# Order of the three matmuls of a split product: per tile, or per piece of weights (one hybrid attention and HGRN2 layer, one Trainium2 core)

## Chip, cores and metric

One core of a Trainium2 chip runs the whole program. The metric is device time in microseconds (us) for one launch, the median of several runs. A difference of 0.2% is about 5.9 us here.

## What is computed

One layer of a bidirectional encoder, 1024 tokens of width 2048, all in float32:

```
u = rmsnorm(h, g_pre)
z = u @ w_in
aq, ak, av, ag, hq, hf_f, hf_b, hv, hg = jnp.split(z, SPLIT_IDX, axis=-1)
...
y = jnp.concatenate([y_att, y_hg], axis=-1).astype(h.dtype) @ w_out
h = h + rmsnorm(y, g_post)
gate = jax.nn.sigmoid((h @ w_pg).astype(f32))
e = (p_l @ w_pp).astype(f32)
h = h + rmsnorm((gate * e).astype(h.dtype), g_ple)
```

Here w_in is 2048 x 9216, w_out and w_pg are 2048 x 2048, w_pp is 256 x 2048. Between the first two products stand a dilated banded attention of 16 heads and a two-directional HGRN2 scan of 8 heads.

## The kernel before

**The split product.** Every large product is made of three matmuls. An activation tile is kept as hi (fp32r) and lo (bf16, the remainder), a weight piece as wh (fp32r), wl (fp32r, the remainder) and wb (bf16). The product is hi·wh + hi·wl + lo·wb, added up in one PSUM bank. Such three matmuls, each of 512 columns, are called a triple below, the two fp32r ones H, the bf16 one B. There are 3392 triples. An H carries its weight load inside its own instruction; a B has an instruction LDWEIGHTS of its own ahead of it.

**The pieces.** `piece` (L74 to L85) loads 128 rows x 512 columns of weights (or 4 x 128 x 128) into raw, and ScalarE makes wh (L82), GpSimd wl (L83, in some pieces VectorE), VectorE wb (L84). raw, wh, wl and wb have three buffers each, so the parts of later pieces are made while TensorE works on earlier ones.

**Who uses pieces.** In `group_parts` (L92 to L106) the weights are the stationary operand: one group makes 128 columns of z for both halves of the tokens, in 4 pieces, and each piece serves 2 halves x 4 k-tiles = 8 triples. It is a generator: it yields after each half, so that attention can put other work between. There are 56 groups, so 224 pieces. In `v_group` (L728 to L741) the tokens' tiles are the stationary operand: 16 pieces per call, with one triple per token tile, 2, 2 and 4 tiles in the first three calls and 8 in the last three. In `gemm` (L798 to L823), which makes w_out, w_pg and w_pp products for half of the tokens, a piece serves 4 token tiles; its last `tail` pieces (1, and 8 in the very last call) are kept back, and then run tile by tile, each tile's bank being read out as soon as it is complete.

**Stages.** First the prenorm, the transposes and the v groups (to about 395 us); then 8 HGRN heads (to about 1270 us), each of 4 groups and a chain of small matmuls that takes turns with VectorE (`hgrn`, L272, L278, L297, L304, L349, L363); then 8 pairs of attention heads (to about 2085 us), each with a k, a q and a gate group and 16 units of scores (L631, L636), softmax (L642 to L650), transposes (L655) and products with v (L539, L553); then w_out, and at last w_pg with w_pp, the second rmsnorm and the output.

**Order.** TensorE runs its instructions in the order of its queue. That order is made when the kernel is built: a scheduler works through the program in the order of its lines with priorities (pieces come early), and puts small matmuls of the chains between the triples of a group where it expects their inputs.

Of the kernel before, what the change touches and what calls it, by code (L numbers as in the profile page):

```python
# [24 lines left out]
KT = 16  # L25
# [19 lines left out]
class Kern:  # L45
# [17 lines left out]

    # ---- weights: a piece [128 (k), 512] in three parts
    def gb(self):
# [20 lines left out]

    # ---- z^T for 128 columns of w_in
    def group(self, *a):
# [3 lines left out]
    def group_parts(self, w_in, c0, sink, halves=(0, 1)):  # L92
        nc = self.nc
        pb = {hf: self.gb() for hf in halves}
        for p in range(4):
            src = w_in[512 * p:512 * p + 512, c0:c0 + 128].rearrange("(k p) c -> p k c", p=128)
            wh, wl, wb = self.piece(src, [4, 128])
            for hf in halves:
                for k in range(4):
                    kt = 4 * p + k  # L100
                    nc.tensor.matmul(pb[hf], wh[:, k], self.uh[hf][:, kt], start=(kt == 0), stop=False)  # L101
                    nc.tensor.matmul(pb[hf], wl[:, k], self.uh[hf][:, kt], start=False, stop=False)  # L102
                    mm = nc.tensor.matmul(pb[hf], wb[:, k], self.ul[hf][:, kt], start=False, stop=(kt == KT - 1))  # L103
                yield mm
        for hf in halves:
            sink(hf, pb[hf])  # L106
# [36 lines left out]

    # ---- split of x^T-like data held in PSUM into hi and lo
    def split_evac(self, hi, lo, p):
# [4 lines left out]

    # ---- phase 0
    def prenorm(self, x, g_pre, pool, tiles):
# [19 lines left out]

    # ---- HGRN2
    def hg_consts(self, lbs, g_hg):
# [50 lines left out]
    def hgrn(self, w_in, h, vsrc, yout):  # L225
# [21 lines left out]

        # ---- intra-chunk scores
        X = big.tile([128, S], F32, name="X", tag="X", bufs=2)
# [13 lines left out]
        n = S  # L263
# [144 lines left out]

    # ---- attention
    def att_consts(self, positions):  # L410
# [292 lines left out]
def tile_hybrid(ctx, tc, x, p, positions, w_in, w_out, g_pre, g_post, g_hg, lb_fwd, lb_bwd, w_pg, w_pp, g_ple, out):  # L703
# [22 lines left out]
    def v_group(cg, toks, pool):  # L726
        c0 = (2048, 2560, 7168, 7680)[cg]
        pb = {t: (K.gb() if t < NGB else K.wk("vb")) for t in toks}  # L728
        for k in range(KT):
            wh, wl, wb = K.piece(w_in[128 * k:128 * k + 128, c0:c0 + 512], [512], prio=False,  # L730
                                 sub=V if len(toks) == 2 and k % 2 else None)
            for t in toks:
                ts = slice(128 * (t % 4), 128 * (t % 4) + 128)
                hi, lo = K.uh[t // 4], K.ul[t // 4]
                nc.tensor.matmul(pb[t], hi[:, k, ts], wh, start=(k == 0), stop=False)  # L735
                nc.tensor.matmul(pb[t], hi[:, k, ts], wl, start=False, stop=False)
                nc.tensor.matmul(pb[t], lo[:, k, ts], wb, start=False, stop=(k == KT - 1))  # L737
        for t in toks:
# [58 lines left out]
    def gemm(w, act, order, c0, sink, tail, bank, pre=None, get=None):  # L797
# [5 lines left out]

        def mm(t, k, pc, first, last):
            ts = slice(128 * t, 128 * t + 128)
            wh, wl, wb = pc
            nc.tensor.matmul(pb[t], hi[:, k, ts], wh, start=first, stop=False)  # L807
            nc.tensor.matmul(pb[t], hi[:, k, ts], wl, start=False, stop=False)  # L808
            nc.tensor.matmul(pb[t], lo[:, k, ts], wb, start=False, stop=last)  # L809

        for j, k in enumerate(order):
            if pre:
                pre(j, k)
            pc = K.piece(w[128 * k:128 * k + 128, c0:c0 + 512], [512], get(j) if get else None)
            if j < n - tail:
                for t in toks:
                    mm(t, k, pc, j == 0, False)
            else:
                pcs.append((k, pc))
        for t in toks:  # L820
            for i, (k, pc) in enumerate(pcs):
                mm(t, k, pc, n == tail and i == 0, i == len(pcs) - 1)
            sink(t, pb[t])  # L823
# [195 lines left out]
```

## Time and profile before

| | |
|---|---|
| runs | 2932.80, 2936.83, 2938.66 us; median 2936.83 |
| profiled execution | its span is 2936.8 us; the profile gives no other time of it |
| TensorE (PE) busy | 2842.3 us, 97% of the span |
| weight loads (PEld) busy | 1684.8 us, 57% |
| VectorE (DVE) busy | 1433.9 us, 49% |
| GpSimd (POOL) busy | 1046.8 us, 36% |
| ScalarE (ACT) busy | 930.2 us, 32% |

A row of the view of groups gives a line of the kernel, the engine, the operation, output<-inputs by the program's names, the shape, how often it occurs, then the busy time, the mean of one in ns, and the idle time of the engine just before them with what ended it. A row of the timeline gives start and duration in us, engine, line and operation; instructions of one line in a row are merged, with their count behind x. Matmuls overlap in these rows, since each row includes the way through the array: what a matmul costs the engine is the distance between the ends (or starts) of two neighbours, not its duration.

### The profile page before, as it was taken

The numbers are of one execution on the slowest core, as the hardware profiler recorded it, in microseconds if no ns is written. First come the engines' busy times: TensorE is split into PE (matmuls) and PEld (weight loads), VectorE is DVE, ScalarE is ACT, GpSimd is POOL, SyncE is SP. The second block draws the span as 40 slices with busy tenths as digits, with TensorE's granted clock in tenths as the row PEclk, the third lists the DMA queues.
The fourth block names the chain that finished last, engine by engine and source line by source line (L and its number), as shares of the span: only waits on it lengthen the run. The fifth ranks groups of instructions, "written<-read, shape, count | busy, mean of one in ns | idle before, by whom it ended". The sixth has DMA issues, their size and how long they took to land. (4 is left out here: it accounts for less than half of the span.)

```text
span 2936.8 us, 46862 instructions
## 1 busy us (share of the span) xinstructions
PE 2842.3 (97%) x18384; PEld 1684.8 (57%) x18384; DVE 1433.9 (49%) x2833; ACT 930.2 (32%) x1676; POOL 1046.8 (36%) x769
## 2 busy tenths in 40 slices
PE   6999999999999999999999999999999999999997
PEld 4555556566566566565555555555555555555554
DVE  8501116756255355356656556565632633543435
ACT  5311112222122122124434434443533223333323
POOL 2422224324314313322222222222244554666555
PEclk9999999999999999999999999999999999999999
DMA  6412221211211111122221222222344543443443
GB/s 229 121 49 76 76 86 37 65 52 37 59 50 40 59 48 41 58 58 62 74 70 43 77 72 56 59 74 70 103 125 127 161 146 94 124 121 108 143 153 113
DMA packets 251613, 250.54 MB, mean 85 GB/s; under 512 B 21632, under 2 KB 175232, under 8 KB 250240
## 3 DMA queue, kind: packets, MB, share of 16 engines
q1 hardware_dynamic: 242224, 238.62, 27.5%
q10 hardware_dynamic: 9168, 8.93, 0.9%
q8 instruction: 144, 2.36, 0.3%
q14 instruction: 77, 0.63, 0.1%
HBM read 205.54 MB, written 29.36 MB: 80 GB/s over the span
## 5 line engine op out<-in xcount | busy, mean ns | idle before, releaser
L83 POOL TENSOR_TENSOR wl<-raw,wh 128x512 fp32r<-128x512 f32 x568 | 786.5, 1389 | 1590.5 <-ACT wh L82 1496.4
L101 PE MATMUL gb<-uh,wh 128*128 128x512 f32 x1792 | 1027.9, 574 | 0.0
L84 DVE CAST wb<-raw 128x512 bf16<-128x512 f32 x584 | 346.8, 598 | 955.7 <-PE gb L103 377.4
L82 ACT CAST wh<-raw 128x512 fp32r<-128x512 f32 x584 | 358.5, 618 | 1190.8 <-PE gb L101 343.9
L102 PE MATMUL gb<-uh,wl 128*128 128x512 f32 x1792 | 711.1, 397 | 1.0 <-POOL wl L83 1.0
L103 PE MATMUL gb<-ul,wb 128*128 128x512 bf16 x1792 | 698.8, 390 | 0.0
L103 PEld LDWEIGHTS <-wb 128*128 128x128 bf16 x1792 | 172.1, 96 | 467.9 <-issue 460.5
L102 PEld LDWEIGHTS gb<-uh,wl 128*128 128x128 f32 x1792 | 340.6, 190 | 44.1 <-POOL wl L83 1.4
L101 PEld LDWEIGHTS gb<-uh,wh 128*128 128x128 f32 x1792 | 358.6, 200 | 3.5 <-issue 1.5
L807 PE MATMUL gb<-wh,yh 128*128 128x512 f32 x512 | 296.1, 578 | 2.9 <-DVE Y L833 2.0
L807 PE MATMUL gb<-wh,th 128*128 128x512 f32 x480 | 277.3, 578 | 0.0
L808 PE MATMUL gb<-wl,yh 128*128 128x512 f32 x512 | 203.5, 398 | 3.2 <-POOL wl L83 3.2
L809 PE MATMUL gb<-wb,yl 128*128 128x512 bf16 x512 | 201.0, 393 | 0.0
L808 PE MATMUL gb<-wl,th 128*128 128x512 f32 x480 | 190.9, 398 | 5.9 <-POOL wl L83 5.7
L809 PE MATMUL gb<-wb,tl 128*128 128x512 bf16 x480 | 187.3, 392 | 0.0
L735 PE MATMUL gb<-wh,uh 128*128 128x512 f32 x256 | 146.6, 579 | 2.1 <-ACT wh L82 2.1
L735 PE MATMUL vb<-wh,uh 128*128 128x512 f32 x256 | 148.4, 580 | 0.0
L647 ACT ACTIVATE asm<-asm,anm 128x512 f32<-128x512 f32 x128 | 92.5, 723 | 147.8 <-DVE anm L645 147.0
L809 PEld LDWEIGHTS <-yl 128*128 128x128 bf16 x512 | 49.3, 96 | 138.0 <-issue 137.7
L737 PEld LDWEIGHTS <-ul 128*128 128x128 bf16 x512 | 49.2, 96 | 137.8 <-issue 137.0
L809 PEld LDWEIGHTS <-tl 128*128 128x128 bf16 x512 | 49.0, 96 | 136.7 <-issue 136.3
L642 DVE CUSTOM_DVE_ANT_1 asm<-asc,amask 128x512 f32<-128x512 f32 x128 | 87.8, 686 | 76.0 <-PE asc L636 75.9
(274 smaller groups left out, 3958.4 us busy)
## 6 DMA issues: line engine op xcount, KB each, us to landing
raw<-in_w_in_dram SPq DMA_DIRECT2D x320, 256.0 KB
raw<-in_w_out_dram SPq DMA_DIRECT2D x128, 256.0 KB
raw<-in_w_pg_dram SPq DMA_DIRECT2D x128, 256.0 KB
xt<-in_x_dram SPq DMA_DIRECT2D x8, 1024.0 KB
vD<-vo SPq DMA_DIRECT2D x32, 256.0 KB
raw<-yD SPq DMA_DIRECT2D x32, 256.0 KB
xr<-in_x_dram SPq DMA_DIRECT2D x32, 256.0 KB
ak<-ak SPq DMA_DIRECT2D x96, 64.0 KB
```

Source lines behind the costliest of these rows:

```text
L82: nc.scalar.copy(wh, raw)
L83: (sub or nc.gpsimd).tensor_tensor(wl, raw, f32(wh), op=ALU.subtract)
L84: nc.vector.tensor_copy(wb, raw)
L101: nc.tensor.matmul(pb[hf], wh[:, k], self.uh[hf][:, kt], start=(kt == 0), stop=False)
L102: nc.tensor.matmul(pb[hf], wl[:, k], self.uh[hf][:, kt], start=False, stop=False)
L103: mm = nc.tensor.matmul(pb[hf], wb[:, k], self.ul[hf][:, kt], start=False, stop=(kt == KT - 1))
L642: V.tensor_tensor_reduce(out=smh.rearrange("p (a b) -> p a b", a=2), in0=sc.rearrange("p (a b) -> p a b", a=2), in1=mk, scale=1.0, scalar= ...
L647: nc.scalar.activation(smh, smh, AF.Exp, bias=nm, accum_out=den)
L735: nc.tensor.matmul(pb[t], hi[:, k, ts], wh, start=(k == 0), stop=False)
L807: nc.tensor.matmul(pb[t], hi[:, k, ts], wh, start=first, stop=False)
L808: nc.tensor.matmul(pb[t], hi[:, k, ts], wl, start=False, stop=False)
L809: nc.tensor.matmul(pb[t], lo[:, k, ts], wb, start=False, stop=last)
```

## The change

In each piece the H of all tiles are issued first, and the B of all tiles behind them. In `group_parts` that makes 16 H and then 8 B; the generator's first yield comes behind 16 H and 4 B, its second behind 4 more B. In `v_group` it makes 2 H per token tile and then one B per tile. In `gemm` it makes 8 H and then 4 B; in the kept-back part each tile runs the H of all kept pieces, and then their B. No instruction is added or taken away, and no operand changes.

```diff
@@ group_parts
             for hf in halves:
                 for k in range(4):
                     kt = 4 * p + k
                     nc.tensor.matmul(pb[hf], wh[:, k], self.uh[hf][:, kt], start=(kt == 0), stop=False)
                     nc.tensor.matmul(pb[hf], wl[:, k], self.uh[hf][:, kt], start=False, stop=False)
+            for hf in halves:
+                for k in range(4):
+                    kt = 4 * p + k
                     mm = nc.tensor.matmul(pb[hf], wb[:, k], self.ul[hf][:, kt], start=False, stop=(kt == KT - 1))
                 yield mm
@@ v_group
             for t in toks:
-                ts = slice(128 * (t % 4), 128 * (t % 4) + 128)
-                hi, lo = K.uh[t // 4], K.ul[t // 4]
-                nc.tensor.matmul(pb[t], hi[:, k, ts], wh, start=(k == 0), stop=False)
-                nc.tensor.matmul(pb[t], hi[:, k, ts], wl, start=False, stop=False)
-                nc.tensor.matmul(pb[t], lo[:, k, ts], wb, start=False, stop=(k == KT - 1))
+                hi = K.uh[t // 4][:, k, 128 * (t % 4):128 * (t % 4) + 128]
+                nc.tensor.matmul(pb[t], hi, wh, start=(k == 0), stop=False)
+                nc.tensor.matmul(pb[t], hi, wl, start=False, stop=False)
+            for t in toks:
+                lo = K.ul[t // 4][:, k, 128 * (t % 4):128 * (t % 4) + 128]
+                nc.tensor.matmul(pb[t], lo, wb, start=False, stop=(k == KT - 1))
@@ gemm
             if j < n - tail:
                 for t in toks:
-                    mm(t, k, pc, j == 0, False)
+                    high(t, k, pc, j == 0)
+                for t in toks:
+                    low(t, k, pc, False)
             else:
                 pcs.append((k, pc))
         for t in toks:
             for i, (k, pc) in enumerate(pcs):
-                mm(t, k, pc, n == tail and i == 0, i == len(pcs) - 1)
+                high(t, k, pc, n == tail and i == 0)
+            for i, (k, pc) in enumerate(pcs):
+                low(t, k, pc, i == len(pcs) - 1)
             sink(t, pb[t])
```

`high` issues the two H of a tile, `low` its B; in the changed kernel the lines below `group_parts` stand 3 lines lower, so L103 becomes L106, L272 becomes L275, and L807 to L809 become L810, L811 and L814.

**First place.** TensorE's queue inside a piece of a group. Before, one half's triples stand one by one (uh and ul are the hi and lo of u for one half of the tokens):

```order
L101 MATMUL gb_3227<-uh1_95,wh_3294 128x512
L102 MATMUL gb_3227<-uh1_95,wl_3295 128x512
L103 LDWEIGHTS wb_3296
L103 MATMUL gb_3227<-ul1_97,wb_3296 128x512
L101 MATMUL gb_3227<-uh1_95,wh_3294 128x512
L102 MATMUL gb_3227<-uh1_95,wl_3295 128x512
L103 LDWEIGHTS wb_3296
L103 MATMUL gb_3227<-ul1_97,wb_3296 128x512
```

Now the same piece has its last H of the second half, then the B of both halves:

```order
L101 MATMUL gb_3227<-uh1_95,wh_3294 128x512
L102 MATMUL gb_3227<-uh1_95,wl_3295 128x512
L106 LDWEIGHTS wb_3296
L106 MATMUL gb_3226<-ul0_96,wb_3296 128x512
L106 LDWEIGHTS wb_3296
L106 MATMUL gb_3226<-ul0_96,wb_3296 128x512
L106 LDWEIGHTS wb_3296
L106 MATMUL gb_3226<-ul0_96,wb_3296 128x512
L106 LDWEIGHTS wb_3296
L106 MATMUL gb_3226<-ul0_96,wb_3296 128x512
L106 LDWEIGHTS wb_3296
L106 MATMUL gb_3227<-ul1_97,wb_3296 128x512
```

What moved: the B of the first half now stand behind all H of both halves. Over the whole queue a B stands directly behind another B 9 times before and 2640 times now.

**Second place.** TensorE's queue at the start of the first HGRN head's chain (pl is the bank of that chain; hq and KD come from ScalarE, VectorE and GpSimd). Before, the chain's first matmuls follow the q group's last triple at once:

```order
L103 LDWEIGHTS wb
L103 MATMUL gb<-ul_97,wb 128x512
L272 MATMUL pl<-hq,KD 32x32 x16
L101 MATMUL gb<-uh_94,wh 128x512
L102 MATMUL gb<-uh_94,wl 128x512
L103 LDWEIGHTS wb
L103 MATMUL gb<-ul_96,wb 128x512
L101 MATMUL gb<-uh_94,wh 128x512
L102 MATMUL gb<-uh_94,wl 128x512
L272 MATMUL pl<-hq,KD 32x32 x16
```

Now three H of the next group come first, and one H instruction pair is split around each batch:

```order
L106 LDWEIGHTS wb
L106 MATMUL gb<-ul_97,wb 128x512
L101 MATMUL gb<-uh_94,wh 128x512
L102 MATMUL gb<-uh_94,wl 128x512
L101 MATMUL gb<-uh_94,wh 128x512
L275 MATMUL pl<-hq,KD 32x32 x16
L102 MATMUL gb<-uh_94,wl 128x512
L101 MATMUL gb<-uh_94,wh 128x512
L275 MATMUL pl<-hq,KD 32x32 x16
```

What moved: the first batch stands three triple matmuls later, the second stands where it stood (five behind the group's end). The later batches of the chain have the same number of triple matmuls between them as before (8, 10, 10, 8, 9, 7, 7), in another mixture of H and B.

**Third place.** TensorE's queue in the very last call of `gemm`, where eight pieces (wx holds their wh and wl, wxb their wb) are kept back. Before:

```order
L807 MATMUL gb<-wx,th_22851 128x512
L808 MATMUL gb<-wx,th_22851 128x512
L809 LDWEIGHTS tl_22852
L809 MATMUL gb<-wxb,tl_22852 128x512
L807 MATMUL gb<-wx,th_22851 128x512
L808 MATMUL gb<-wx,th_22851 128x512
L809 LDWEIGHTS tl_22852
L809 MATMUL gb<-wxb,tl_22852 128x512
```

Now the first tile's last kept piece, with the start of the B behind it:

```order
L810 MATMUL gb<-wx,th_22851 128x512
L811 MATMUL gb<-wx,th_22851 128x512
L814 LDWEIGHTS tl_22852
L814 MATMUL gb<-wxb,tl_22852 128x512
L814 LDWEIGHTS tl_22852
L814 MATMUL gb<-wxb,tl_22852 128x512
```

What moved: all 8 B of a tile now stand behind the H of the eighth kept piece; before, 7 of them stood ahead of it.

## Rows read from the trace of the kernel before

**Rows 1.** The page's first part, and TensorE's and its clock's line by 40 slices.

```profile
PE 2842.3 (97%) x18384; PEld 1684.8 (57%) x18384; DVE 1433.9 (49%) x2833; ACT 930.2 (32%) x1676; POOL 1046.8 (36%) x769
...
PE   6999999999999999999999999999999999999997
...
PEclk9999999999999999999999999999999999999999
```

**Rows 2.** Stages (us from:to, length, then busy time of each engine and count).

```profile
0.00:100.00 100.00, 71.78 (x330) 45.27 (x331) 81.48 (x146) 55.96 (x95) 33.33 (x28) 0.95 0.61 203
...
395.00:1270.00 875.00, 858.66 (x7639) 533.64 (x7638) 451.31 (x884) 185.40 (x306) 276.19 (x197) 1.00 0.18 52
1270.00:2145.00 875.00, 864.04 (x5876) 506.88 (x5877) 522.52 (x1140) 384.73 (x706) 215.35 (x157) 1.00 0.25 70
2145.00:2937.00 792.00, 752.77 (x3271) 430.18 (x3267) 334.66 (x539) 259.06 (x495) 442.63 (x326) 0.98 0.43 129
```

**Rows 3.** Timeline of PE inside a group, 1000 to 1012 us (start, duration).

```profile
1000.63 0.39 PE L103 MATMUL gb<-ul,wb 128*128 128x512 bf16 x1
1000.67 0.58 PE L101 MATMUL gb<-uh,wh 128*128 128x512 f32 x1
1001.09 0.40 PE L102 MATMUL gb<-uh,wl 128*128 128x512 f32 x1
1001.32 0.39 PE L103 MATMUL gb<-ul,wb 128*128 128x512 bf16 x1
1001.36 0.58 PE L101 MATMUL gb<-uh,wh 128*128 128x512 f32 x1
...
1011.76 0.58 PE L101 MATMUL gb<-uh,wh 128*128 128x512 f32 x1
```

**Rows 4.** Timeline of weight loads (PEld) in the same stretch.

```profile
1001.32 0.10 PEld L103 LDWEIGHTS <-wb 128*128 128x128 bf16 x1 [0.27 <-issue]
1001.32 0.20 PEld L101 LDWEIGHTS gb<-uh,wh 128*128 128x128 f32 x1
1001.55 0.19 PEld L102 LDWEIGHTS gb<-uh,wl 128*128 128x128 f32 x1
```

**Rows 5.** Timeline of PE and PEld at three H in a row, 86.0 to 87.6 us.

```profile
86.22 0.39 PE L737 MATMUL gb<-wb,ul 128*128 128x512 bf16 x1
86.25 0.81 PE L735 MATMUL gb<-wh,uh 128*128 128x512 f32 x2
86.91 0.40 PE L736 MATMUL gb<-wl,uh 128*128 128x512 f32 x1
87.15 0.39 PE L737 MATMUL gb<-wb,ul 128*128 128x512 bf16 x1
...
86.22 0.42 PEld L735 LDWEIGHTS gb<-wh,uh 128*128 128x128 f32 x2
86.68 0.19 PEld L736 LDWEIGHTS gb<-wl,uh 128*128 128x128 f32 x1
```

**Rows 6.** Timeline of PE where two B stand in a row, in gemm.

```profile
2083.83 0.61 PE L809 MATMUL gb<-wb,yl 128*128 128x512 bf16 x2
...
2613.79 0.39 PE L809 MATMUL gb<-wb,tl 128*128 128x512 bf16 x1
...
2614.49 0.60 PE L809 MATMUL gb<-wb,tl 128*128 128x512 bf16 x2
```

**Rows 7.** Whom PE waited for: us in total, times, longest.

```profile
PE pu L363 <- DVE hk L349: 5.1, 8, 1.1
PE pa L297 <- DVE Q L278: 4.5, 5, 1.3
PE pl L272 <- DVE Q L278: 3.9, 8, 0.5
```

**Rows 8.** The page's chain that ended last, by engine.

```profile
PE 14%; DVE 2%; POOL 1%; DMA 1%; issue 1%; ACT 0%; SPq 0%; DVEq 0%; POOLq 0%; ACTq 0%
```

**Rows 9.** Timeline of PE in the kept-back part of the last gemm.

```profile
2903.98 0.51 PE L808 MATMUL gb<-wx,th 128*128 128x512 f32 x1 [0.89 <-POOL wx L83]
2904.32 0.39 PE L809 MATMUL gb<-wxb,tl 128*128 128x512 bf16 x1
2904.36 0.59 PE L807 MATMUL gb<-wx,th 128*128 128x512 f32 x1
```

More of the change, by code (lines that the diff above doesn't have):

```diff
@@ L802, in gemm, with high, low @@
         pcs = []
[L804 to L809, printed above, removed]
+        def high(t, k, pc, first):
+            a = hi[:, k, 128 * t:128 * t + 128]
+            nc.tensor.matmul(pb[t], a, pc[0], start=first, stop=False)
+            nc.tensor.matmul(pb[t], a, pc[1], start=False, stop=False)
+        def low(t, k, pc, last):
+            nc.tensor.matmul(pb[t], lo[:, k, 128 * t:128 * t + 128], pc[2], start=False, stop=last)
         for j, k in enumerate(order):
```

## The prediction
> **What bounds the kernel now.** I looked at the share of busy time first. TensorE is busy 97% of the span, in nearly every slice, and its granted clock stays at the top level, 2.4 GHz [rows 1]; the others are at half or less. A busy TensorE is not one at its peak, because rows of matmuls overlap. So the second view is the table by stage: TensorE lacks 28 us in the first 100 us, 16 us in the HGRN heads, 11 us in the attention, 39 us in w_out and w_pg [rows 2]. Elsewhere its own pace sets the time, and the question becomes what one matmul costs behind another.
>
> That is read from the timeline of TensorE inside a group [rows 3]. From the L101 that starts at 1000.67 to the one at 1011.76 there are 16 triples, 11.09 us, so 0.693 us a triple, with no wait in it. The ends split it: L101 ends at 1001.25, L102 at 1001.49, L103 at 1001.71, the next L101 at 1001.94. So H behind H, B behind H and H behind B each take about 0.23 us. Three kinds of step occur, and a fourth, B behind B, hardly ever. The change replaces steps "H behind B" and "B behind H" by "H behind H" and "B behind B".
>
> **The price of the two new steps.** B behind B: nine cases exist, and two are shown. A merged row of two takes 0.61 or 0.60 us where a single B takes 0.39 [rows 6], so the second costs 0.21 to 0.22 us; I take 0.215. H behind H: it is in every triple, but always with a B next. Once three H stand in a row without a wait: the B ahead ends at 86.61, the third H at 87.31 [rows 5], 0.70 us for three, so 0.233 each. With 0.01 us of rounding in that row the H lies between 0.230 and 0.237. I take the middle.
>
> The weight loads tell why B is cheaper behind B [rows 4]: the load of a B is recorded as starting at the same moment as its matmul, 0.27 us after the loads before it, while the H's load (0.20 us) starts when the matmul ahead of it does. I read this as the H being paced by its own load, and the B behind an H by a load that is not pulled ahead. Behind another B it seems to be.
>
> The Trainium skill, page "TensorE: Matmul & The Clock Gate", section "Back-to-back issue gap", gives 512 columns / 2.4 GHz + 2.5 ns, 0.216 us, for a matmul behind a matmul, whatever stands ahead. The B behind B agrees with it; the other three steps of this trace do not. By that rule alone a triple would take 0.648 us in either order, and the sum of this part would be nothing.
>
> **The sum, part by part.** A block is one piece's run: n triples that were n x 0.693 us. Now its first triple still has one H behind a B and one B behind an H, so it keeps its price; each further triple adds two H behind H and one B: 2 x 0.233 + 0.215 = 0.681 us, so 12 ns less. How many further triples there are follows from the loops: groups 224 pieces x 7 = 1568; v groups 48 x 7 + 16 x 3 + 32 x 1 = 416; gemm 241 pieces x 3 + 4 x 7 = 751; together 2735. Chains cut some blocks: the queue shows 2640 B behind a B in place of 9, so 2631 further triples count. **2631 x 12 ns = 31.6 us** of TensorE's own time.
>
> Against that stand four places where the gain does not reach the end.
> - The first 100 us. TensorE waits 28 us there for data [rows 2]; the 80 further triples of the small v groups (1.0 us) are counted as nothing.
> - The HGRN chains. VectorE and TensorE take turns, and TensorE waits for VectorE 21 times, 13.5 us in all [rows 7]; between those batches stand about 31 of a head's 128 triples. Where TensorE waits, a shorter fill only makes the wait longer. The heads' gain is 8 x 16 pieces x 7 x 12 ns = 10.8 us; 24% of it, 2.6 us, is lost. The first batch of a chain stands three matmuls later, the second where it was, so I price that move at nothing: the later batches decide.
> - w_out and w_pg. The chain of waits reaches back over the last fifth, and about 5 of its 19 hundredths are not TensorE [rows 8]. The gain there is 751 x 12 ns = 9.0 us; a quarter, 2.2 us, is lost.
> - The end of the last gemm. The first tile's eighth kept piece arrives at 2903.98 us, after a wait for GpSimd [rows 9]. Before, one B followed it; now eight do, so 7 x 0.215 = 1.5 us of work that filled the earlier waits comes after the arrival. All tiles behind it shift by that.
>
> Losses 1.0 + 2.6 + 2.2 + 1.5 = 7.3 us. **31.6 - 7.3 = 24.3 us.** The sum is against the profiled execution, span 2936.8 us, which is also the median of the runs: **2912.5 us**.
>
> What I cost at nothing: the first half's bank of a group is complete 4 B (0.9 us) before the second's instead of 12 matmuls (2.8 us). Its read-out is hidden, since the next group has two other banks; without that cover it would cost up to 1.9 us per group. The buffers of wh and wl come free after two thirds of a piece instead of at its end, wb's not; no queue is moved past anything there. In attention the fills between score units become uneven (5 to 18 matmuls where they were 9 to 19); TensorE lacks only 11 us there [rows 2], and a unit's transposes stand two units behind its scores, which hides it. The waits that a bad case would add are in the range.
>
> With H behind H at 0.230 a further triple takes 0.675 us, the gain is 2631 x 18 ns = 47 us, and with the same losses the time is 2897. At 0.237 it is 0.689, 10.5 us less 7.3: 2934.
>
> **Rivals.**
> - *Weight loads become the bound (slower).* An H load takes 0.19 to 0.20 us, twice a B's 0.10 [rows 4]; in a run of 16 H no short load comes between. For: only three H in a row are on record. Two loads there take 0.42 us, and 0.04 us passes before the third [rows 5]; if from the fourth on this gap were no longer hidden, an H would take 0.21 + 0.04 = 0.25 us. Then a further triple takes 0.715, 22 ns more than now: 2631 x 22 ns = 58 us, 2995 us. It decides from an H of 0.239 us upwards. Against: the third H in the row is no slower than the first two, and loads there are 0.23 us apart, the pace of the matmuls. The Trainium skill, same page, "Weight-path perf modes", says that the fast weight load is off for FP32 weights; the loads of 0.20 against 0.10 us agree. **8%.**
> - *The order is indifferent (no change).* If B behind B is cheap only where something else delayed the pair, 0.23 stays for all, and the sum is nothing: 2937 us, give or take the 1.5 us of the end. By the skill's issue gap quoted above it would be the same, for another reason: there would be nothing to gain. Against: both merged rows show it [rows 6]. **8%.**
> - *The chains take more.* If everything gained in the HGRN heads and in w_out and w_pg goes into waits, 31.6 - 1.0 - 10.8 - 9.0 - 1.5 = 9.3 us is left: 2927.5 us. For: in both stages the waits are there; against: most of a head's triples stand in unbroken groups. **14%.**
> - That the change does not do what it says is ruled out by the queue: the B stand behind each other 2640 times.
>
> **How the numbers follow.** My forecast has 70%, with 2898 to 2922 us as its own spread. What a measurement can tell from no change is 0.2%, 5.9 us. Forecast and third rival are faster by more: 84%. The indifferent order is within: 8%. The load bound is slower: 8%. The range reaches from the forecast's lower bound across the third rival, 2898 to 2930 us; it leaves out the two other rivals and the ends of the H price.
>
> **What would show it.** In the profile after: 16 H in a row with ends 0.233 us apart and B with ends 0.215 apart; a piece of a group, 16 H and 8 B, of about 5.46 us where it took 5.55; TensorE's busy time lower by about 30 us; waits of L297, L363 and L272 (three lines lower) longer by 2 to 3 us together; TensorE's last matmul ending about 1.5 us later behind the eighth kept piece. H ends 0.24 us or more apart would prove me wrong, and so would B ends 0.23 us apart; a correct pace with an unchanged time would mean that the waits have grown.

## The result and the profile after

The changed kernel took 2902.74 to 2911.69 us in four runs, median **2908.45 us**, beside 2937.74 us for the kernel before: ratio 0.9899, interval 0.9882 to 0.9916. That is 29.3 us faster; 24.3 us were forecast. The profiled execution is the slowest of the four; it has a span of 2909.9 us, against 2936.8 us before, so the two traces differ by 26.9 us, and this has to be found in them.

First the page's busy times after, against [rows 1]:

```profile
PE 2785.7 (96%) x18128; PEld 1885.7 (65%) x18384; DVE 1508.4 (52%) x2833; ACT 925.5 (32%) x1672; POOL 1023.8 (35%) x769
```

TensorE's busy time is lower by 56.6 us, twice what the span gained. Part of that is only the record: 18128 of 18384 matmuls are in this trace, and the 256 missing ones are B. So the price of a step is better read where the rows are whole, in one piece of a group:

```profile
1002.63 0.58 PE L101 MATMUL gb<-uh,wh 128*128 128x512 f32 x1
1003.05 0.39 PE L102 MATMUL gb<-uh,wl 128*128 128x512 f32 x1
...
1004.43 0.39 PE L102 MATMUL gb<-uh,wl 128*128 128x512 f32 x1
...
1006.24 0.39 PE L102 MATMUL gb<-uh,wl 128*128 128x512 f32 x1
1006.47 1.90 PE L106 MATMUL gb<-ul,wb 128*128 128x512 bf16 x8
1008.02 0.58 PE L101 MATMUL gb<-uh,wh 128*128 128x512 f32 x1
```

From the first L101 to that of the next piece are 5.39 us, where eight triples took 8 x 0.693 = 5.55 us [rows 3] and 5.46 us were forecast. The eighth H ends at 1004.82, the 16th at 1006.63. From the first end, 1003.21, that makes 7 steps of 0.230 us and then 8 of 0.226. The B: (1.90 - 0.39) / 7 = 0.216 us. So B behind B is as forecast, and **an H behind an H gets cheaper along the row**: 0.233 us in the old triple [rows 3], 0.230 up to the eighth place, 0.226 behind it. (A short row of 3 H, the only one there was before [rows 5], could not show that.) It is the place in the row, not the half of the tokens that the later eight H work on: in blocks of 8 H (the shorter rows below) the second half's H are as dear as the first's, 0.231 us on average, and in rows of 32 the 17th to 32nd, which serve both halves of the next piece, take 0.227 us. The Trainium skill, page "TensorE: Matmul & The Clock Gate", section "Back-to-back issue gap", gives 512 / 2.4 GHz + 2.5 ns, 0.216 us, as the gap of a single matmul, and about 0.131 us for a long stream of them with their weight loads; the B agree with the first number, the H come nearer to it in a long row but do not reach it, and no step of these rows is below 0.215 us.

In gemm a further triple costs 2 x 0.230 + 0.216 = 0.676 us, so a piece of four saves 3 x 0.017 = 0.05 us. TensorE's own saving, an estimate from these rows, is then 272 pieces of eight x 0.16 = 43.5 us (224 of groups, 48 of v groups), and some 12 us for the 751 further triples of gemm. About 2 us go off for blocks that a chain cuts: **some 53 us** instead of the forecast 31.6.

Where did the other half go? The stages after, with the columns of [rows 2]:

```profile
0.00:100.00 100.00, 71.11 (x321) 45.81 (x327) 80.23 (x141) 55.95 (x95) 33.12 (x28) 0.97 0.60 202
395.00:1260.00 865.00, 834.51 (x7554) 599.13 (x7641) 461.25 (x900) 186.94 (x306) 257.48 (x197) 1.00 0.18 52
1260.00:2125.00 865.00, 848.77 (x5798) 561.96 (x5875) 488.03 (x1125) 381.53 (x704) 215.88 (x159) 1.00 0.25 71
2125.00:2910.00 785.00, 737.12 (x3175) 477.82 (x3233) 428.99 (x538) 254.99 (x492) 438.44 (x323) 0.98 0.43 130
```

Length less TensorE's busy time is 28.9, 30.5, 16.2 and 47.9 us, where it was 28.2, 16.3, 11.0 and 39.2. A part of that growth is only the record: a single missing B leaves a hole of 2 x 0.216 - 0.39 = 0.04 us, and 87 of them are missing in the heads. What each stretch kept is told by four events that both programs have: the first batch (L272, now L275) of the first and of the last HGRN chain, the end of the last product of attention, and the end of TensorE's work. Timeline of TensorE, before:

```profile
475.15 0.46 PE L272 MATMUL pl<-hq,KD 128*32 128x32 f32 x32
1242.34 0.46 PE L272 MATMUL pl<-hq,KD 128*32 128x32 f32 x32
2144.82 0.82 PE L553 MATMUL ao<-aPT,avn 128*64 128x128 f32 x10
2921.12 0.39 PE L809 MATMUL gb<-wxb,tl 128*128 128x512 bf16 x1
```

After:

```profile
467.07 0.46 PE L275 MATMUL pl<-hq,KD 128*32 128x32 f32 x32
1225.98 0.46 PE L275 MATMUL pl<-hq,KD 128*32 128x32 f32 x32
2118.83 0.71 PE L556 MATMUL ao<-aPT,avn 128*64 128x128 f32 x8
2892.46 1.90 PE L814 MATMUL gb<-wxb,tl 128*128 128x512 bf16 x8
```

| stretch | before | after | kept | TensorE saved |
|---|---|---|---|---|
| to the first chain | 475.15 | 467.07 | 8.1 | about 9.6 (48 v pieces and 12 of the first head x 0.16) |
| 7 HGRN heads | 767.19 | 758.91 | 8.3 | 7 x 16 x 0.16 = 17.9 |
| last head's rest, attention | 903.30 | 893.56 | 9.7 | about 16.6 (100 pieces x 0.16, and 12 of w_out x 0.05) |
| w_out, w_pg | 775.87 | 774.82 | 1.0 | about 11.4 |

The stretch before the chains kept most of it, the heads less than half, attention a little over half, and the last stage almost nothing. The waits that grew stand in the view of whom TensorE waited for (us in total, times, longest; those of the chain, pl, pu and pa, answer to [rows 7]):

```profile
PE gb L811 <- POOL wl L83: 10.1, 7, 4.0
PE pl L275 <- DVE Q L281: 8.8, 16, 0.9
PE pu L366 <- DVE hk L352: 8.2, 8, 1.2
PE pa L275 <- DVE Q L281: 4.7, 7, 0.7
...
PE ao L542 <- DVE aPT L664: 3.1, 1, 3.1
PE asc L634 <- issue: 2.4, 2, 2.3
PE pa L300 <- DVE Q L281: 1.7, 7, 0.3
```

In the chains TensorE now waits 8.8 + 8.2 + 4.7 + 1.7 = 23.4 us for VectorE, where it was 13.5: 10 us more, and 2 to 3 were forecast.

### The profile page after: what moved, and what is told of

The parts are those of the page before. It is cut to its first block, busy times and chain, and to the rows that moved or that the text cites. A ratio compares the mean times of both kernels' runs of the same rounds, so it can differ in the third digit from the quotient of the medians.

```text
span 2909.9 us, 46582 instructions
## 1 busy us (share of the span) xinstructions
PE 2785.7 (96%) x18128; PEld 1885.7 (65%) x18384; DVE 1508.4 (52%) x2833; ACT 925.5 (32%) x1672; POOL 1023.8 (35%) x769
## 5 line engine op out<-in xcount | busy, mean ns | idle before, releaser
L84 DVE CAST wb<-raw 128x512 bf16<-128x512 f32 x584 | 430.5, 740 | 785.2 <-PE gb L106 281.8
L101 PE MATMUL gb<-uh,wh 128*128 128x512 f32 x1792 | 744.3, 415 | 0.0
L106 PE MATMUL gb<-ul,wb 128*128 128x512 bf16 x1632 | 405.7, 380 | 9.8 <-issue 1.8
L101 PEld LDWEIGHTS gb<-uh,wh 128*128 128x128 f32 x1792 | 337.1, 188 | 82.9 <-issue 1.2
L106 PEld LDWEIGHTS <-wb 128*128 128x128 bf16 x1792 | 158.4, 98 | 204.6 <-issue 54.3
L810 PE MATMUL gb<-wh,yh 128*128 128x512 f32 x512 | 231.2, 452 | 2.8 <-DVE Y L842 2.8
L810 PE MATMUL gb<-wh,th 128*128 128x512 f32 x480 | 215.8, 450 | 0.0
L811 PE MATMUL gb<-wl,yh 128*128 128x512 f32 x512 | 203.7, 398 | 4.7 <-POOL wl L83 4.7
L811 PE MATMUL gb<-wl,th 128*128 128x512 f32 x480 | 190.6, 397 | 5.4 <-POOL wl L83 5.4
L814 PE MATMUL gb<-wb,yl 128*128 128x512 bf16 x479 | 133.7, 383 | 1.6
L814 PE MATMUL gb<-wb,tl 128*128 128x512 bf16 x452 | 126.2, 384 | 1.0
L810 PEld LDWEIGHTS gb<-wh,yh 128*128 128x128 f32 x512 | 97.6, 191 | 33.3 <-DVE Y L842 3.3
L811 PEld LDWEIGHTS gb<-wl,yh 128*128 128x128 f32 x512 | 97.4, 190 | 24.3 <-POOL wl L83 5.9
L738 PE MATMUL gb<-wl,uh 128*128 128x512 f32 x256 | 102.4, 407 | 10.9 <-POOL wl L83 7.9
L634 PE MATMUL asc<-ak,aqt 128*32 128x256 bf16 x1536 | 109.7, 401 | 3.2 <-issue 2.4
```

The costliest lines, as they stand in the source:

```text
L84: nc.vector.tensor_copy(wb, raw)
L634: t = nc.tensor.matmul(sc[32 * r:32 * r + 32, :256], qb[:, sq, 32 * r:32 * r + 32], KS[s][:, h, r::4], start=(s == 0), stop=False, skip_gr ...
L738: nc.tensor.matmul(pb[t], hi, wl, start=False, stop=False)
L810: nc.tensor.matmul(pb[t], a, pc[0], start=first, stop=False)
L811: nc.tensor.matmul(pb[t], a, pc[1], start=False, stop=False)
L814: nc.tensor.matmul(pb[t], lo[:, k, 128 * t:128 * t + 128], pc[2], start=False, stop=last)
```

## Experiments

All ratios are to the kernel before, run on the same chip. Three questions were open: which of the three edited functions brings what, what takes the gain back in the HGRN heads and in the last stage, and whether another length of the rows is better.

**Groups alone.** Only `group_parts` is new; `v_group` and `gemm` are those of before.

```diff
@@ group_parts, as in the change
+            for hf in halves:
+                for k in range(4):
+                    kt = 4 * p + k
                     mm = nc.tensor.matmul(pb[hf], wb[:, k], self.ul[hf][:, kt], start=False, stop=(kt == KT - 1))
                 yield mm
```

> Only group_parts has the new order; v_group and gemm run triple by triple as before. Theory 1 (the gain reaches the end in the v stage and in attention, half of it in the HGRN heads, and almost none of it in w_out and w_pg, because waits grow there): without the v groups (48 large pieces, about 6.3 us by the stage times of the two traces) and without gemm (about 1 us) some 22 us of the 29 remain, 2916 us, ratio to before 0.9925. Rival (each further triple gives the same 29.3 us / 2735 = 10.7 ns wherever it stands): 1568 x 10.7 ns = 16.8 us, 2921 us, ratio 0.9943.

Measured: 2918.55 us, 0.9937 (0.9924 to 0.9949). The numbers of both theories lie inside the interval, so the total decides nothing between them. The periods of the heads and of the attention pairs are those of the full change, so the gain of these stages, and its loss, belong to the groups.

**Gemm alone.** `group_parts` and `v_group` of before, `gemm` of after.

```diff
@@ gemm, as in the change
-                    mm(t, k, pc, j == 0, False)
+                    high(t, k, pc, j == 0)
+                for t in toks:
+                    low(t, k, pc, False)
```

> Only gemm has the new order. Theory 1 (TensorE's saving in w_out and w_pg turns into waits): 0 to 2 us, 2936 to 2938 us, ratio 0.9993 to 1.0000; the distance from the first to the second batch of transposes and the rest up to the end is as before. Rival (the same 10.7 ns for each of its 751 further triples): 8 us, 2930 us, ratio 0.9973.

Measured: 2934.37 us over 11 runs, 0.9989 (0.998 to 0.9997), 1 to 6 us faster. The rival's number, 0.9973, is outside; of the first theory's range (0.9993 to 1) only the near end is inside. In gemm half or more of the 12 us is lost, by the median about 8 us, even without the new groups ahead of it.

**The v groups alone.** Only `v_group` is new.

```diff
@@ v_group, as in the change
-                nc.tensor.matmul(pb[t], lo[:, k, ts], wb, start=False, stop=(k == KT - 1))
+            for t in toks:
+                lo = K.ul[t // 4][:, k, 128 * (t % 4):128 * (t % 4) + 128]
+                nc.tensor.matmul(pb[t], lo, wb, start=False, stop=(k == KT - 1))
```

> Only v_group has the new order. Theory 1 (the v stage is TensorE's own pace, so its saving reaches the end whole): the chain of the first HGRN head begins about 6 us earlier than before, 2932 us, ratio 0.9979; and the three parts done alone (groups 18.5 us, gemm 3 us, v 6 us) add up to the change's 29 us. Rival (what the v stage saves is waited for later): ratio 0.9995 to 1.

Measured: 2929.62 us, 0.9971 (0.9959 to 0.9982). The first chain's first batch starts at 468.42 us, 6.7 us earlier than before, and the end is 7.5 us earlier by the medians (2937.14 us before, on that chip): what is won ahead of the chains stays won. The three parts add up: 0.63 + 0.11 + 0.29 = 1.03% of gain, against 1.01% for the whole.

**No subtraction on GpSimd in the heads.**

```diff
@@ piece, while the HGRN heads are built
             nc.scalar.copy(wh, raw)
-            (sub or nc.gpsimd).tensor_tensor(wl, raw, f32(wh), op=ALU.subtract)
+            if self.light:
+                nc.scalar.copy(wl, raw)
+            else:
+                (sub or nc.gpsimd).tensor_tensor(wl, raw, f32(wh), op=ALU.subtract)
```

> The changed kernel, but in the groups of the HGRN heads wl is a plain copy of raw made by ScalarE in place of GpSimd's subtraction: the subtraction is left out there, and GpSimd has less to do. TensorE's queue is the same, row for row. Theory 1 (the chain of a head is VectorE at work without a gap, and an instruction of VectorE that runs beside GpSimd's wl takes about 1 us more; the changed kernel has three such meetings in a chain, 2.5 us): the long VectorE instructions of the chain (1.78, 2.03 and 1.94 us in one head) are back at 0.69, 1.28 and 1.29 us, and the period of a head falls from 108.4 us by 1 to 2.5 us. Rival (the chain got longer because TensorE's batches stand elsewhere in its queue): the instructions may get shorter, the period stays within 0.4 us of 108.4.

Measured, in one run: 2884.85 us. This kernel leaves out the remainder that wl is, so it is not a faster layer; it is of use for its rows alone. The timeline of TensorE shows the first and the last chain:

```profile
465.00 0.46 PE L280 MATMUL pl<-hq,KD 128*32 128x32 f32 x32
1206.50 0.46 PE L280 MATMUL pl<-hq,KD 128*32 128x32 f32 x32
```

That is 741.50 / 7 = 105.93 us per head, where the changed kernel has 108.42 and the kernel before 109.60; TensorE's own saving alone would have made 109.60 - 16 x 0.16 = 107.04. So the loss is gone, and some of what was there before with it. What happens is seen in VectorE's groups of the chain in the HGRN stage (count, busy us, mean ns, then VectorE's idle us just ahead of them). Before:

```profile
L278 DVE TENSOR_TENSOR Q<-Q,TB 128x512 f32<-128x512 f32 x96 | 65.6, 723 | 1.7 <-PE pa L304 1.1 <-PE pa L297 0.2
L278 DVE TENSOR_TENSOR X<-X,TB 128x512 f32<-128x512 f32 x48 | 36.0, 750 | 0.0
```

After:

```profile
L281 DVE TENSOR_TENSOR Q<-Q,TB 128x512 f32<-128x512 f32 x96 | 73.0, 798 | 3.2 <-PE pa L307 2.0 <-PE pa L300 1.0
L281 DVE TENSOR_TENSOR X<-X,TB 128x512 f32<-128x512 f32 x48 | 41.4, 862 | 0.0
```

With the wl made by ScalarE:

```profile
L286 DVE TENSOR_TENSOR Q<-Q,TB 128x512 f32<-128x512 f32 x96 | 63.5, 708 | 2.6 <-PE pa L312 1.9 <-PE pa L305 0.5
L286 DVE TENSOR_TENSOR X<-X,TB 128x512 f32<-128x512 f32 x48 | 33.5, 697 | 0.0
```

VectorE's idle time ahead of 96 instructions is 2 to 3 us in all: it works through the chain almost without a gap, so each instruction that takes longer moves the chain. The change made these two groups longer by 7.4 + 5.4 = 12.8 us, 1.6 us per head; per head 1.4 us of TensorE's 2.56 us was lost. One chain of the changed kernel shows when it happens. VectorE in the fourth head:

```profile
798.38 1.78 DVE L281 TENSOR_TENSOR X<-X,TB 128x512 f32<-128x512 f32 x1
...
802.62 0.68 DVE L281 TENSOR_TENSOR X<-X,TB 128x512 f32<-128x512 f32 x1
...
804.22 1.29 DVE L281 TENSOR_TENSOR Q<-Q,TB 128x512 f32<-128x512 f32 x2
...
807.03 2.03 DVE L281 TENSOR_TENSOR Q<-Q,TB 128x512 f32<-128x512 f32 x2
```

and GpSimd beside it:

```profile
797.88 1.73 POOL L83 TENSOR_TENSOR wl<-raw,wh 128x512 fp32r<-128x512 f32 x1 [6.38 <-ACT wh L82]
805.97 1.94 POOL L83 TENSOR_TENSOR wl<-raw,wh 128x512 fp32r<-128x512 f32 x1 [6.37 <-ACT wh L82]
```

An X beside a wl takes 1.78 us, alone 0.68; a pair of Q 2.03 against 1.29. GpSimd waits as well: the first wl is recorded from 797.88 us on, while VectorE's Q ahead of that X still runs (797.77 to 798.46), and takes 1.73 us where it takes 1.27 with VectorE out of its way. The Trainium skill, page "SBUF — State Buffer", section "SBUF: two separate sides", says that a VectorE instruction with two SBUF inputs and a GpSimd instruction that reads SBUF share a port pair, which whichever starts first holds for its whole length. The rows agree in that one waits out the other; who holds the pair, the recorded starts do not always tell (a row of the next experiment). In the changed kernel 24 of these 144 Q and X take over 0.9 us, three in each head, all of them beside a wl that had started; before there were 8, one in each head, and without the subtraction in the heads 2.

**The gate group in the old order.** The gate group follows a head's chain in the program and fills the chain's waits; here it alone keeps its triples, all else is as in the change.

```diff
@@ group_parts(..., triples=False)
+                    if triples:
+                        mm = nc.tensor.matmul(pb[hf], wb[:, k], self.ul[hf][:, kt], start=False, stop=(kt == KT - 1))
+                if triples:
+                    yield mm
-            for hf in halves:
+            for hf in () if triples else halves:
@@ hgrn
-        self.group(w_in, base + 4096, lambda hf, p: self.gate_evac(gt[:, 512 * hf:512 * hf + 512], p))
+        self.group(w_in, base + 4096, lambda hf, p: self.gate_evac(gt[:, 512 * hf:512 * hf + 512], p), (0, 1), True)
```

> The changed kernel, but the gate group of each HGRN head, the one that fills TensorE's queue between the batches of the chain, runs triple by triple as before (32 of 224 pieces). Theory 1 (the chain is paced by VectorE; what the fill saves goes into waits, and the new mixture even costs 0.3 us a head): no slower than the changed kernel, up to 3 us faster, and the stretch from the first batch of the chain to its last (30.4 us a head in the changed kernel, 30.1 before) is back at 30.1. Rival (the fill's saving counts as any other): 32 pieces x 0.14 us = 4.5 us slower than the changed kernel, ratio to before 0.9914.

Measured: 2899.42 us, 0.9872 (0.9856 to 0.9888): 9 us below the changed kernel by the medians, though the two intervals overlap; up to 3 us were expected. The mechanism is seen without that. A head takes 107.50 us; with 12 of its 16 pieces in the new order TensorE's saving alone gives 109.60 - 12 x 0.16 = 107.68. The chain, from its first batch to its last, takes 29.3 us in most heads, where it took 30.4 in the changed kernel and 30.1 before. The seven periods make 6.4 us of the 11.1 us between the two spans; 3.4 us more lie in w_out and w_pg, whose code is the same in both. And VectorE's rows are short again:

```profile
L285 DVE TENSOR_TENSOR Q<-Q,TB 128x512 f32<-128x512 f32 x96 | 66.0, 725 | 2.0 <-PE pa L304 0.9 <-PE pa L311 0.7
L285 DVE TENSOR_TENSOR X<-X,TB 128x512 f32<-128x512 f32 x48 | 34.7, 724 | 0.0
```

When a piece's buffers come free sets when GpSimd starts the next wl. With the old order in this one group 8 of the 144 Q and X are long, not 24. In the fourth head it is GpSimd that waits, while VectorE works on through six instructions:

```profile
806.23 5.12 POOL L83 TENSOR_TENSOR wl<-raw,wh 128x512 fp32r<-128x512 f32 x1 [7.21 <-ACT wh L82]
```

What changed is when the two meet, and which of them waits. The gain is timing, not a rule: it is read from the rows.

**Shorter rows.** Each half of a piece in 8 H and 4 B.

```diff
@@ group_parts
-            for hf in halves:
                 for k in range(4):
                     kt = 4 * p + k
                     mm = nc.tensor.matmul(pb[hf], wb[:, k], self.ul[hf][:, kt], start=False, stop=(kt == KT - 1))
```

> The changed kernel, but in a group each half makes its 8 H and then its 4 B (blocks of 4 triples in place of 8), as in gemm. Theory 1 (the step H behind H falls along a row: 0.231 us on average for the first eight places, 0.227 from the ninth): 1344 further triples of 15.4 ns, 20.7 us of TensorE's time, where blocks of 8 give about 31; three quarters of the difference reach the end, so about 8 us slower than the changed kernel, ratio to before 0.9926. Rival (one price for every step, 12 ns for a further triple): 224 further triples fewer, 2.7 us, ratio 0.9908.

Measured: 2911.04 us, 0.9911 (0.9897 to 0.9924). The rival's number, 0.9908, is met; 0.9926 lies just outside. But the reason behind 0.9926 holds: half a piece takes 2.72 us (from the L101 at 1000.78 to the one at 1003.50), 5.44 for a piece, not 5.39. A head takes 108.96 us against 108.42, an attention pair 101.56 against 101.07. The head lost about 1.1 us here too (109.60 - 16 x 0.11 would be 107.84), though none of its Q and X is long: the wl meet other instructions of VectorE instead: the O take 44.1 us against 35.4, 1.1 us a head, and the casts 127.3 against 58.0. So the rows of Q and X alone do not tell what a chain loses. It is given back elsewhere: the wait of 2.3 us at the first scores (below) is not there, and w_out with w_pg takes some 4 us less.

**Longer rows.** Two pieces together: 32 H, then 16 B.

```diff
@@ group_parts
-        for p in range(4):
+        for p2 in range(2):
+            pcs = []
+            for p in (2 * p2, 2 * p2 + 1):
...
+                pcs.append((p, self.piece(src, [4, 128])))
+            for p, (wh, wl, wb) in pcs:
...
             for hf in halves:
-                for k in range(4):
+                for p, (wh, wl, wb) in pcs:
+                    for k in range(4):
```

> The changed kernel, but a group makes the 32 H of two pieces and then their 16 B. Theory 1 (an H costs 0.227 us from the ninth place of a row on): the second piece's first eight H save 4 ns each and one change of kind to the other is saved (18 ns), 50 ns x 112 = 5.6 us of TensorE's time; in attention, where the saving reaches the end, the period of a head pair falls from 101.07 us by 0.3; in the HGRN heads nothing. 2 to 4 us faster than the changed kernel, unless the fills, now in one kind for longer, delay a chain. Rival (a step's price has nothing to do with its place in the row): 112 x 18 ns = 2 us of TensorE's time, the H step by place is flat after the second.

Measured: 2911.89 us, 0.9915 (0.9902 to 0.9929), no better than one piece, where 2 to 4 us of gain were expected. The longer rows are cheaper: an attention pair takes 100.23 us against 101.07, more than the 0.3 us expected. In the heads it does not arrive: in the shortest periods a head takes 76.9 us outside the chain against 77.9, and the chain 31.3 against 30.4, but the mean of the seven periods is 109.26 us against 108.42. And the wait for ao where attention ends is 3.3 us.

**A fourth buffer for wb,** since wb is now the part that is held longest.

```diff
-                wb = self.wp.tile([128] + shape, BF16, name="wb", tag="wb", bufs=3)
+                wb = self.wp.tile([128] + shape, BF16, name="wb", tag="wb", bufs=4)
```

> The changed kernel with four buffers for wb in place of three. Theory 1 (the waits that grew in w_out and w_pg come from VectorE: a wb buffer now comes free only with a block's last B, so its cast runs while GpSimd makes wl and takes 0.74 us on average in place of 0.60): the mean cast is back near 0.6 us, and the changed kernel gets 3 to 6 us faster, ratio to before 0.988. Rival (the casts have slack; the waits are for wl on GpSimd and for the banks): the casts may get shorter, the time stays within 2 us of the changed kernel, ratio 0.990.

Measured: 2920.89 us, 0.9935 (0.9922 to 0.9947), slower than the change; neither theory had that. VectorE's casts in w_out and w_pg got shorter, as hoped. Before, after, and with four buffers (one row of the view of groups each):

```profile
L84 DVE CAST wb<-raw 128x512 bf16<-128x512 f32 x249 | 150.4, 608 | 323.5 <-PE gb L809 283.8 <-DMA raw<-in_w_pg_dram 28.1 <-DMA raw<-in_w_out_dram 6.9
```

```profile
L84 DVE CAST wb<-raw 128x512 bf16<-128x512 f32 x248 | 241.8, 978 | 255.3 <-PE gb L814 207.3 <-DMA raw<-in_w_pg_dram 19.7 <-PE gb L811 15.0
```

```profile
L84 DVE CAST wb<-raw 128x512 bf16<-128x512 f32 x246 | 206.3, 840 | 305.4 <-PE gb L814 126.7 <-DMA raw<-in_w_out_dram 73.2 <-DMA raw<-in_w_pg_dram 69.3
```

The last stage is 2.7 us shorter with it, but attention 9.5 us longer: the scheduler, which works with when buffers come free, interleaved attention another way (in most pairs 13 H where 11 stood between two batches of scores). That this is what costs the 9.5 us is likely, not shown. A size that the scheduler sees is no clean experiment.

**Gemm: all wh, then all wl, then all wb.** GpSimd's wl comes last of a piece's parts in the waits, so it is asked for later.

```diff
@@ gemm
-                for t in toks:
-                    high(t, k, pc, j == 0)
+                for i in range(2):
+                    for t in toks:
+                        high(t, k, pc, j == 0, (i,))
```

> The changed kernel, but in gemm a piece's four wh matmuls come first, then its four wl matmuls, then its four B. Theory 1 (TensorE waits in w_out and w_pg for wl, which GpSimd finishes 1.3 us after wh): three more matmuls, 0.7 us, cover each such wait; the waits on wl there (10 us in 7 waits of over 0.15 us in the changed kernel) fall to a few, 4 to 8 us faster than the changed kernel, ratio to before 0.988. Rival (the stage is paced by the arrival of pieces or by the read-out, a wait only moves): within 2 us of it, 0.990.

Measured: 2904.33 us, 0.9883 (0.987 to 0.9897); the interval overlaps the change's, so a gain is not shown. The waits for wl went from 10.1 us in 7 to 6.3 in 5:

```profile
PE gb L811 <- POOL wl L83: 6.3, 5, 2.4
```

That row has to be read with care: three kernels with the gemm of the change show 7.7 us in 7 (the gate group in triples), 7.1 in 5 (no subtraction in the heads) and 7.2 in 5 (shorter rows), and their w_out with w_pg takes 771 us, as here. What is clear of this spread are VectorE's casts there: 783 ns on average, where the kernels with the gemm and the buffers of the change show 954 to 978.

**Gemm: wb, then wh, then wl,** in the kept-back part too.

```diff
@@ gemm
-                for t in toks:
-                    high(t, k, pc, j == 0)
-                for t in toks:
-                    low(t, k, pc, False)
+                for t in toks:
+                    low(t, k, pc, j == 0)
+                for i in range(2):
+                    for t in toks:
+                        high(t, k, pc, i, False)
```

> The changed kernel, but in gemm a piece's four B come first, then its four wh, then its four wl matmuls; in the kept-back part too. Theory 1: wb needs no GpSimd, so wl is covered by eight matmuls, 1.8 us: the waits on wl vanish, and in the very last call the eighth kept piece is followed by one matmul of its tile in place of eight B (1.5 us): 6 to 11 us faster than the changed kernel, ratio to before 0.987. Rival (VectorE's cast, queued behind the chain of the second rmsnorm, is later than wl was): waits for wb take the place, no faster, 0.990 or above.

Measured: 2902.87 us, 0.9876 (0.9862 to 0.9889), where 6 to 11 us below the change were expected; this interval overlaps the change's too. The waits for wl fell to 3.5 us, and in the kept-back part a new one came, for VectorE's wxb:

```profile
PE gb L809 <- DVE wxb L84: 5.4, 5, 2.3
PE gb L812 <- POOL wl L83: 3.5, 4, 1.1
```

**The two edits together.** The gate group in triples, and gemm by wh, wl, wb:

```diff
@@ hgrn
-        self.group(w_in, base + 4096, lambda hf, p: self.gate_evac(gt[:, 512 * hf:512 * hf + 512], p))
+        self.group(w_in, base + 4096, lambda hf, p: self.gate_evac(gt[:, 512 * hf:512 * hf + 512], p), (0, 1), True)
@@ gemm
-                for t in toks:
-                    high(t, k, pc, j == 0)
+                for i in range(2):
+                    for t in toks:
+                        high(t, k, pc, j == 0, (i,))
```

> The changed kernel with both edits that were faster alone: the gate group of each HGRN head triple by triple, and in gemm wh, wl, B. Theory 1 (they lie in different stages and add): 9 us from the first, 4 us from the second, about 2895 us, ratio 0.9855. Rival (they don't add; the last stage is paced by the arrival of pieces): 0.9872, as with the first alone.

Measured: 2898.16 us, 0.9867 (0.985 to 0.9883). Both theories' numbers, 0.9855 and 0.9872, lie inside: whether the gemm order adds to the gate group's gain isn't decided. With wb first instead, and the first tile of the kept-back part in (wb, wh, wl) piece by piece, so that little is left behind the last arrival:

```diff
@@ gemm, kept-back part
+            if t == 0:
+                steps = [(i, m) for m in range(len(pcs)) for i in (2, 0, 1)]
+            else:
+                steps = [(i, m) for i in (2, 0, 1) for m in range(len(pcs))]
```

> As the run before, but in gemm B, wh, wl, and in the kept-back part the first tile goes piece by piece, so that one piece's three matmuls follow the last arrival. Theory 1 (the 5.4 us that TensorE waited for wxb in the kept-back part with B first fall away): 2 to 4 us faster than wh, wl, B: 2892 us, ratio 0.9843. Rival (those waits only stood in place of waits for wx): the same as wh, wl, B, 0.9855.

Measured: **2894.01 us** (2891.77 to 2899.56), 0.9853 (0.9836 to 0.9869). It is the fastest kernel that leaves nothing out, 43 us below the one before, and of the waits for wxb 0.2 us is left. Both theories' numbers, 0.9843 and 0.9855, lie inside. Its interval overlaps that of the kernel ahead of it; against the change itself (0.9882 to 0.9916) it does not.

## Why the prediction was right, and where its sum was not

The direction, the mechanism and the time were right. But that the sum landed near the result is luck: two of its terms were too small by similar amounts, TensorE's own saving (31.6 us, by the rows about 53) and the losses (7.3 us; about 53 less the 27 that the trace kept, so about 26).

- **B behind B at 0.215:** right, 0.216.
- **H behind H at 0.233:** the term that was mis-sized. "The H lies between 0.230 and 0.237. I take the middle" rested on a row of three; 0.230 was the bound, and from the ninth place on 0.226 is below it. Per piece the saving is 0.16 us, not 0.084.
- **The load bound** did not come: no place of a long row is on average dearer than the 0.233 us of the triple. That the order is indifferent is excluded by the total.
- **The first 100 us:** right, TensorE lacks 28.9 us there, 28.2 before. And what the v groups won afterwards arrived nearly whole, which v groups alone shows.
- **The HGRN chains, 24% lost:** the share of a head's triples that stand between the chain's batches, 31 of 128, was taken as the measure. In fact 17.9 - 8.3 = 9.6 us of 17.9 was lost in the seven periods, more than half, and for a reason the prediction did not have: VectorE, which sets the chain's pace, was held up beside GpSimd's wl in three of its Q and X in each head, where it was in one before. The kernel without that subtraction shows it: the loss is gone. About two thirds of the loss lie inside the chain (30.4 us where it was 30.1, though its 31 triples should have saved 0.6 us); where the rest goes was not located. The sentence "VectorE and TensorE take turns" missed that VectorE has hardly a gap.
- **Attention's unevenness at nothing:** wrong at its edges. Inside, nearly all arrives: the scores of the second pair start at 1431.46, of the last at 2037.87, 101.07 us a pair where it was 102.89, 1.82 of 12 x 0.16 = 1.92 us. But the first scores now stand eight matmuls later, behind the generator's fifth yield, and two waits are new, in the timeline of TensorE:

```profile
1330.40 0.86 PE L634 MATMUL asc<-ak,aqt 128*32 128x256 bf16 x12 [2.28 <-issue]
2083.00 3.36 PE L542 MATMUL ao<-aPT,avc 128*64 128x128 f32 x29 [3.13 <-DVE aPT L664]
```

- **w_out and w_pg, a quarter lost:** in this trace 10 of about 11 us was. The waits for wl became fewer and longer (longest 2.1 us before, 4.0 after). VectorE's casts went from 608 to 978 ns; as many as before lie beside a wl of GpSimd (168, now 174), but these now take 1.18 us instead of 0.66: 154 casts take over 0.9 us, and for 137 of them the wl had started first; before it was 26 of 44. And behind long waits TensorE's granted clock is 0.50, the lower of the two levels, 1.2 GHz. Between 1300 and 2880 us eight such stretches stand, four before. What each of the three costs was not separated, and the cause of this loss stays open: with the same gemm code this stage took 765.7 to 774.8 us in six kernels, so the 1.0 us that the change kept there is the low end of a spread.
- **The kept-back part at 1.5 us:** the mechanism was right, the size not, again by the clock. Where one B stood behind the last arrival [rows 9], TensorE's rows now are:

```profile
2873.55 0.79 PE L811 MATMUL gb<-wx,th 128*128 128x512 f32 x1 [0.21 <-POOL wx L83]
2874.14 3.64 PE L814 MATMUL gb<-wxb,tl 128*128 128x512 bf16 x8
```

and the stretches there (clock third from the end):

```profile
2866.00:2872.00 6.00, 2.55 (x7) 0.97 (x6) 2.36 (x3) 1.91 (x4) 5.01 (x4) 0.93 0.35 111
2872.00:2878.00 6.00, 5.67 (x12) 2.54 (x13) 0.34 (x1) 0.28 (x2) 1.37 (x2) 0.50 0.00 0
```

The eighth piece comes at 2873.55, and its tile's 8 B take 3.64 us where 8 B at the full clock took 1.90. TensorE had worked only 2.55 of the 6 us ahead, and the granted clock was 0.50 in the 6 us that follow. So the price is about 1.5 us for the work that stands behind the arrival, and 1.7 us more for the clock. From the start of the eighth piece's last H to TensorE's end it is 20.8 us now (2873.55 to 2894.36), and 17.5 us before (2903.98 to 2921.51): 3.3 us more, which agrees.
- **The signs named in advance:** ends 0.233 apart was too much, 0.216 was right, a piece at 5.46 was 5.39, waits in the chain longer by 10 us instead of 2 to 3. "A correct pace with an unchanged time would mean that the waits have grown" is what happened to half of the gain.

## What to carry to other kernels

Price a reordering of matmuls by the distance between ends of neighbours of each kind, and where the trace holds only short rows of a kind, let the range reach below the shortest row's price. Before counting a TensorE saving as time, ask in each stage which engine has no gaps: there the saving goes into waits, and an earlier free buffer can start work on GpSimd right beside VectorE's critical instructions. Which part of a piece is used first changes whom TensorE waits for, but no such order alone was clear of the change in time here. Keep as little as can be behind the last arrival. And compare kernels whose code in a stage is the same before a difference in that stage is put down to an edit: here they differ by up to 9 us.

## What was not expected of the hardware

- An fp32r matmul of 512 columns behind its like takes 0.230 us up to the eighth place and 0.226 from the ninth; with 32 in a row the H stay there, and the attention pair fell by another 0.84 us. Why the place in the row matters isn't known from these runs.
- VectorE's X beside GpSimd's subtraction takes 1.78 us instead of 0.68, and the subtraction itself 1.73 to 1.94 us, where it takes 1.27 us after the chain (at 828.35 us). Either can be the one that waits: in the heads of the kernel before four wl are recorded at 7.5 us, with VectorE at work all through them.
- A wait of 2 to 4 us can cost more than itself. Behind the waits at 1330.40 and 2083.00 us, and one of 3.98 us at 2287.68, TensorE's granted clock is 0.50 for the next 3 us, and behind the last of them H follow each other at 0.43 us:

```profile
1332.00:1335.00 3.00, 2.78 (x31) 1.14 (x21) 1.71 (x7) 2.89 (x5) 1.28 (x1) 0.50 0.16 38
2083.00:2086.00 3.00, 3.00 (x28) 3.00 (x30) 0.69 (x1) 0.56 (x1) 0.00 (x0) 0.50 0.47 135
2287.60:2290.80 3.20, 3.12 (x7) 2.15 (x7) 3.20 (x3) 0.45 (x1) 3.13 (x3) 0.50 0.42 131
```
